# Thresholds of query blocks 3 and 4 by a bit search on ScalarE in a hybrid sparse and sliding-window decoder layer

## Chip, cores and metric

The kernel runs on one core of a Trainium2 chip. The metric is the device time of one execution in microseconds, as the median of several runs. The engines are TensorE (PE, with its weight loads PEld), VectorE (DVE), ScalarE (ACT), GpSimd (POOL) and SyncE (SP), which issues the loads.

## What is computed

One decoder layer of width 1024 over 1024 tokens with 16 meta tokens in front: a SwiGLU FFN as a half step, then a sparse and a sliding-window attention in parallel, merged by sigmoid gates, then a second SwiGLU FFN. The part that the change touches is the selection of keys in the sparse branch. For each query an indexer scores all admissible keys, and attention runs over the 256 best:

```python
def one_block(args):
    qa_b, qi_b, wi_b, qpos = args
    rel = relu(einsum('bqhd,bsd->bqhs', qi_b, ki))
    score = einsum('bqhs,bqh->bqs', rel, wi_b)
    score = where(admissible, score, NEG_INF)
    top_val, top_idx = lax.top_k(score, topk)      # topk = 256
    ...
    s = where(sel_ok, s, NEG_INF); p = softmax(s)
```

The kernel doesn't gather the selected keys. It turns each block's scores into a bias, 0 for a selected key and -1e30 for any other, and adds it to the attention scores of all keys.

## The kernel before

Queries are cut into eight blocks b = 0 to 7 of 128 rows; block b sees w = 16 + 128 (b + 1) keys, so block 3 has 528 columns and block 4 has 656. After the first FFN a middle stage runs in this program order. For each half x of the tokens: keys (`k_half`), indexer queries (`q_groups`), values (`v_half`), the scores of the half's blocks (`score`, L763), the sliding-window queries, and the four sliding-window blocks (`swa_block`, L897), each of which ends with the product `o` (L884) and the transposed tile `oT` (L891, L892). Then come the sparse queries, the search for the thresholds of blocks 5 to 7 (`search`, L796), and the sparse blocks 0 to 7 (`sparse_block`, L954), with eight calls of `swa_merge` between them, each of which computes gates and the sliding-window branch (tiles `p_gate`, `p_br`) and writes two merged tiles `mg` (L1029). After sparse block 7 the sparse gates and the output projection of both halves follow (`p_gate`, `p_br`, `p_out`).

There are two ways to the bias of a block:

- `by_max` (L784 to L794), for blocks 1 to 4, on DVE alone. A round takes the 8 largest scores of each row (MAX8, L790) and overwrites them by a mark (MATCH_VALUE_LOAD and MATCH_REPLACE8, L791). Blocks 1 and 2 drop their smallest scores in 2 and 18 rounds; blocks 3 and 4 mark their 256 largest in 32 rounds each. One last instruction (L792) turns marks into the bias.
- `search` (L796 to L848) and `select` (L850 to L864), for blocks 5 to 7 together. The search finds each row's 256th largest score bit by bit. A round counts on ACT how many scores exceed a trial value: a Sign with the trial as bias and an accumulator, one for each block (L812). Then three small integer instructions on DVE compare the count (`d`, L815), set the bit (`key`, L829) and make the next trial (`nb`, L827). There are 32 rounds, the sign bit among them, and a closing count on DVE (L837). The 16-bit output of the Signs is not used; it goes to the scratch tile `jk`, of which there is one. `select` then makes the bias from the scores and the threshold in eight DVE instructions (L856 to L864), with two tiles for flags, `gt` (which has the scratch tile's buffer) and `eq`.

The order of instructions in this middle stage is not written out by hand. A scheduler of the framework places them, engine by engine: a work item that comes earlier in the program goes first when its inputs are ready by the scheduler's own reckoning. On the chip each engine then runs its list strictly in order, and waits on semaphores. Buffers of one tag are handed out in program order.

Of the kernel before, what the change touches and what calls it, by code (L numbers as in the profile page):

```python
# [9 lines left out]
F16 = mybir.dt.float16  # L10
# [6 lines left out]
P = 128  # L17
# [4 lines left out]
T = META + SEQ  # L22
# [33 lines left out]
def layer_kernel(ctx: ExitStack, tc: tile.TileContext, xT, gains, wgu1, wd1, win, wvi, wbs, wbw, wout,  # L56
# [5 lines left out]
    ph = {}  # L62
# [787 lines left out]
    def select(b, kth):  # L850
        w = META + P * (b + 1)
        raw = sc[b][0]
        gt = ph["sb"].tile([P, T], F16, tag="jk", name="gt", bufs=1)[:, :w]
        eq = ph["sb"].tile([P, T], F16, tag="eq", name="eq", bufs=1)[:, :w]
        room = small(8, "room")[:, 0:1]
        nc.vector.tensor_scalar(out=gt, in0=raw, scalar1=kth, scalar2=None, op0=ALU.is_gt, op1=ALU.add,  # L856
                                accum_out=room)
        nc.vector.tensor_scalar(room, room, -1.0, float(TOPK), op0=ALU.mult, op1=ALU.add)
        nc.vector.tensor_scalar(eq, raw, kth, None, op0=ALU.is_equal)
        nc.vector.tensor_tensor_scan(eq, eq, eq, 0.0, op0=ALU.add, op1=ALU.bypass)  # L860
        nc.vector.tensor_scalar(eq, eq, room, None, op0=ALU.is_le)
        nc.vector.scalar_tensor_tensor(eq, raw, kth, eq, op0=ALU.is_equal, op1=ALU.mult)
        nc.vector.tensor_add(eq, eq, gt)
        nc.vector.tensor_scalar(raw, eq, -1.0, -NEG, op0=ALU.add, op1=ALU.mult)  # L864
# [122 lines left out]
    def new_oT():  # L987
        return ph["sb"].tile([P, 2, 4, 512], F16, tag="oT", name="oT", bufs=3)
# [12 lines left out]
        return gt, pb  # L1001

    oT_w = []
    for x in range(2):
        k_half(x)
        qi += q_groups((x,), 2, 1)
        if x == 0:
            mix_norm(1, norm_stats(acc, SUB_ALL[1]))
        v_half(x)
        for b in range(4 * x, 4 * x + 4):  # L1010
            if b:
                score(b)
        qs += q_groups((x,), 4, 2)
        oT_w.append(new_oT())
        for b in range(4 * x, 4 * x + 4):
            swa_block(b, qs, oT_w[x])
# [1 line left out]

    vm_sp = v_meta(lambda hh: 0)
    oT_s = [new_oT()]  # L1020
    kth = search((5, 6, 7))
    merged = [[], []]

    def swa_merge(d):
# [12 lines left out]
    swa_merge(0)  # L1037
    swa_merge(1)
    swa_merge(2)
    by_max(3)  # L1040
    sparse_block(3, qa, oT_s[0])
    swa_merge(3)
    by_max(4)
    oT_s.append(new_oT())
    swa_merge(4)
    swa_merge(5)
# [16 lines left out]
    for x in range(2):  # L1063
        mT = []
        for d in range(KD):
            gw, bw = load_w(win[20 + d], 1024), load_w(wbs[d], 512)
            mt = hp([P, 2, 512], F16, "mt")
            gt, pb = gated(x, gw, bw, oT_s[x])
# [11 lines left out]
        for d in range(KD):  # L1080
            w = load_w(wout[d], 1024)
# [120 lines left out]
```

## Time and profile before

| what | value |
|---|---|
| median of three runs | 2032.15 us (2031.77 to 2035.65) |
| profiled execution | 2033.16 us, span of its instructions 2031.1 us |
| mean granted TensorE clock | 0.988 of full speed |
| PE, DVE, ACT, POOL busy | 95%, 80%, 44%, 19% of the span |

The span is what the profile cuts into stages; the rest of the execution, 2 us, lies around it. Busy time is the union of an engine's instructions. The middle stage reaches from about 680 us to 1400 us; the first FFN lies ahead of it and the second behind. In the rows below, `L812` is line 812 of the kernel, `out<-in` are tiles by the program's names, and `128x528` is partitions by columns.

### The profile page before, as it was taken

What the parts mean: (1) busy time and instruction counts of PE and PEld (TensorE: products, weight loads), DVE (VectorE), ACT (ScalarE), POOL (GpSimd) and SP (SyncE); (2) the same over time, 40 slices, a digit from 0 to 9 for tenths busy, and PEclk for the clock granted to TensorE, in tenths of its full rate; (3) what the DMA queues carried; (4) which work ended last, traced back from release to release, by engine and by line L of the source; (5) the groups of instructions that cost most, each with busy time, mean ns of one, the idle gap of its engine ahead of it and who ended that gap; (6) DMA issues with size and microseconds to landing.
All of it is one profiled execution on the core that took longest, in us unless ns stands there. A gap on an engine that the chain in (4) does not pass through costs nothing.

```text
span 2031.1 us, 32839 instructions
## 1 busy us (share of the span) xinstructions
PE 1936.5 (95%) x13080; PEld 1197.3 (59%) x13080; DVE 1627.2 (80%) x2779; ACT 901.0 (44%) x1602; POOL 386.9 (19%) x313
## 2 busy tenths in 40 slices
PE   5899999999999989899999999998899999999997
PEld 4588888888888556454545654444344444444443
DVE  7888788778875799999999964566987787788767
ACT  4433233333323446589885643433433243233232
POOL 3611312221310132221001000002322212312200
PEclk9999999999999999999999999999999999999998
DMA  4011111111113543212020024241112121111213
GB/s 158 11 63 48 58 63 50 55 64 58 48 63 105 183 141 112 99 59 73 17 63 17 27 68 156 78 164 49 34 55 68 48 72 47 63 62 47 76 38 130
DMA packets 58873, 146.95 MB, mean 72 GB/s; under 512 B 7264, under 2 KB 13408, under 8 KB 58720
## 3 DMA queue, kind: packets, MB, share of 16 engines
q1 hardware_dynamic: 58720, 144.86, 22.3%
q8 instruction: 102, 1.67, 0.3%
q14 instruction: 51, 0.42, 0.1%
HBM read 130.01 MB, written 14.76 MB: 71 GB/s over the span
## 4 chain that ended last, share of the span: by engine, by line
PE 70%; DVE 18%; ACT 4%; issue 4%; DMA 2%; POOL 2%; DVEq 0%; SPq 0%; ACTq 0%; POOLq 0%
PE pc L327 14%; PE pd L327 14%; PE pa L327 14%; PE pb L327 7%; PE p_br L999 2%; DVE sc L791 2%; DVE u L222 2%; DVE wsp L131 1%; PE p_gate L147 1%; PE p_gate L145 1%; PE p_gate L146 1%; DVE m L790 1%; PE p_out L146 1%; PE p_out L147 1%; PE p_out L145 1%
## 5 line engine op out<-in xcount | busy, mean ns | idle before, releaser
L327 PEld LDWEIGHTS <-wsp 128*128 128x128 f16 x4176 | 410.0, 98 | 214.2 <-issue 12.3
L327 PEld LDWEIGHTS <-x 128*128 128x128 f16 x3132 | 307.3, 98 | 157.9 <-issue 8.5
L327 PE MATMUL pa<-u,wsp 128*128 128x264 f16 (+1 forms) x1440 | 224.7, 310 | 0.0
L131 DVE SCALAR_TENSOR_TENSOR wsp<-wst,wsp 128x1024 f16<-128x1024 f32 (+2 forms) x130 | 134.8, 1038 | 54.6 <-ACT wsp L130 54.3
L130 ACT ACTIVATE wsp<-wst 128x1024 f16<-128x1024 f32 (+2 forms) x130 | 111.7, 863 | 140.1 <-PE p_out L147 45.9
L147 PEld LDWEIGHTS <-wsp 128*128 128x128 f16 x912 | 90.5, 99 | 94.5 <-issue 12.3
L145 PEld LDWEIGHTS <-wsp 128*128 128x128 f16 x912 | 91.0, 100 | 85.1 <-issue 4.1
L146 PEld LDWEIGHTS <-wsp 128*128 128x128 f16 x912 | 90.7, 99 | 80.2 <-issue 3.9
L327 PE MATMUL pb<-tb,wsp 128*128 128x264 f16 (+1 forms) x720 | 113.7, 312 | 8.1 <-ACT tb L235 5.5
L327 PE MATMUL pc<-tb,x 128*128 128x264 f16 (+1 forms) x720 | 113.9, 313 | 6.6 <-DVE c L458 6.4
L327 PE MATMUL pc<-tb,wsp 128*128 128x256 f16 (+1 forms) x720 | 114.2, 314 | 0.0
L327 PE MATMUL pd<-tb,x 128*128 128x256 f16 (+1 forms) x720 | 110.7, 308 | 0.0
L327 PE MATMUL pd<-u,x 128*128 128x256 f16 (+1 forms) x720 | 110.7, 308 | 0.0
L289 POOL TENSOR_TENSOR t<-g,g 128x512 f32<-128x512 f32 x16 | 25.5, 1595 | 436.0 <-DVE g L494 436.0
L812 ACT ACTIVATE jk<-sc,s5nb 128x784 f16<-128x784 f32 (+2 forms) x93 | 97.9, 1052 | 19.0 <-DVE s5nb L827 15.3
L341 ACT ACTIVATE wsp<-sa 128x1024 f16<-128x1024 f32 (+1 forms) x62 | 60.2, 971 | 103.4 <-DVE sa L393 103.4
L327 PE MATMUL pa<-hid,wsp 128*128 128x264 f16 (+1 forms) x648 | 103.1, 310 | 0.0
L341 ACT ACTIVATE wsp<-wst 128x1024 f16<-128x1024 f32 (+1 forms) x62 | 59.9, 967 | 94.3 <-DMA wst<-in_wgu_dram 49.9
L327 PE MATMUL pd<-hid,x 128*128 128x256 f16 (+1 forms) x648 | 101.6, 308 | 0.0
L147 PE MATMUL p_gate<-u,wsp 128*128 128x512 f16 x256 | 97.0, 379 | 1.4 <-DVE wsp L131 1.4
L145 PE MATMUL p_gate<-u,wsp 128*128 128x512 f16 x256 | 97.0, 379 | 0.0
L146 PE MATMUL p_gate<-u,wsp 128*128 128x512 f16 x256 | 97.0, 379 | 0.0
(234 smaller groups left out, 4147.6 us busy)
## 6 DMA issues: line engine op xcount, KB each, us to landing
wst<-in_wgu_dram SPq DMA_DIRECT2D x88, 512.0 KB, 3.7
wst<-in_win_dram SPq DMA_DIRECT2D x44, 512.0 KB, 3.5
wst<-in_wd_dram SPq DMA_DIRECT2D x48, 384.0 KB, 3.4
wst<-in_wd_dram SPq DMA_DIRECT2D x32, 256.0 KB, 2.7
wst<-in_wout_dram SPq DMA_DIRECT2D x16, 512.0 KB, 4.1
qscr<-ry SPq DMA_DIRECT2D x20, 256.0 KB, 2.1
q<-qscr SPq DMA_DIRECT2D x20, 256.0 KB, 3.0
wst<-in_wbs_dram SPq DMA_DIRECT2D x16, 256.0 KB, 2.7
```

The costliest lines, as they stand in the source:

```text
L130: nc.scalar.activation(sp[:, 0, :n], st[:, :n], AF.Copy, scale=WS)
L131: nc.vector.scalar_tensor_tensor(sp[:, 1, :n], st[:, :n], WS, sp[:, 0, :n], op0=ALU.mult, op1=ALU.subtract)
L145: nc.tensor.matmul(ps, w[:, 0, wcols], xt[:, 0, xcols], start=start, stop=False)
L146: nc.tensor.matmul(ps, w[:, 0, wcols], xt[:, 1, xcols], start=False, stop=False)
L147: nc.tensor.matmul(ps, w[:, 1, wcols], xt[:, 0, xcols], start=False, stop=stop)
L222: nc.vector.tensor_sub(u[k][:, 1, s0:s1], t[:, :w], u[k][:, 0, s0:s1])
L289: nc.gpsimd.tensor_sub(vb(t1), vb(b1), va(a1)[:, :, :wb])
L327: nc.tensor.matmul(ps[:, s, :n], w[:, a, wc], tiles[k][:, y, s * stride:s * stride + n], start=start and k == 0 and j == 0, stop=stop and ...
L341: nc.scalar.activation(sp[:, 0, :n], st[:, :n], AF.Copy, scale=WS)
L791: nc.vector.match_replace(out=raw, in_to_replace=m8, in_values=raw, imm_value=MARK)
L812: nc.scalar.activation(junk[:, :w], sc[b][0], AF.Sign, bias=bias[:, j:j + 1], accum_out=s[:, j:j + 1])
L999: nc.tensor.matmul(pb, bw[:, a, c * P:(c + 1) * P], oT[:, y, c, :], start=c == 0 and n == 0, stop=c == 3 and n == 2)
```

## The change

Blocks 3 and 4 get their thresholds by `search`, one search for each block, called right behind the block's scores. `by_max(3)` and `by_max(4)` are replaced by `select` with these thresholds, at the same places of the program. The flag tile `gt` gets a buffer of its own. Blocks 0 to 2 and 5 to 7 are computed as before. Lines behind the second piece move down by one, those behind the third by three.

```diff
     def select(b, kth):
         w = META + P * (b + 1)
         raw = sc[b][0]
-        gt = ph["sb"].tile([P, T], F16, tag="jk", name="gt", bufs=1)[:, :w]
+        gt = ph["sb"].tile([P, T], F16, tag="gt", name="gt", bufs=1)[:, :w]
...
     oT_w = []
+    kth = {}
...
             if b:
                 score(b)
+                if b in (3, 4):
+                    kth.update(search((b,)))
...
-    kth = search((5, 6, 7))
+    kth.update(search((5, 6, 7)))
...
-    by_max(3)
+    select(3, kth[3])
     sparse_block(3, qa, oT_s[0])
     swa_merge(3)
-    by_max(4)
+    select(4, kth[4])
     oT_s.append(new_oT())
```

The scheduler makes new lists for every engine. Three places show what moves.

**DVE, sliding-window blocks of the second half, around one output `o` (L884).** `m_3` and `m_4` are the 8 largest of blocks 3 and 4, whose scores are `sc_8207` and `sc_9243`; `s5` stands for the search of blocks 5 to 7, `s4` for that of block 4. Before:

```order
L875 TENSOR_TENSOR pts<-ptr,pts 128x512
L815 TENSOR_TENSOR s5d<-s5S,s5thr 128x3
L131 SCALAR_TENSOR_TENSOR wsp<-wst,wsp 128x512
L829 SCALAR_TENSOR_TENSOR s5key<-s5d,s5key 128x3
L791 MATCH_REPLACE sc_8207<-m_3_11877,sc_8207 128x528
L884 TENSOR_TENSOR o<-pv_s,a_rec 128x512
L827 SCALAR_TENSOR_TENSOR s5nb<-s5key,s5flip 128x3
L790 MAX m_3_11880<-sc_8207 128x8
L791 MATCH_REPLACE sc_9243<-m_4_12327,sc_9243 128x656
```

and now:

```order
L912 ISA psw,a_mx<-ps_s,msk_7682,snk_7688 128x256
L912 ISA a_mx 128x1
L815 TENSOR_TENSOR s4d<-s4S,s4thr 128x1
L884 TENSOR_TENSOR o<-pv_s,a_rec 128x512
L829 SCALAR_TENSOR_TENSOR s4key<-s4d,s4key 128x1
L827 SCALAR_TENSOR_TENSOR s4nb<-s4key,s4flip 128x1
```

Between the same kinds of instructions, the small steps of block 4's search stand where rounds of MAX8 and MATCH_REPLACE stood. In the list of the changed kernel all 32 rounds of block 3 and 31 of block 4 stand ahead of the last of these eight outputs. Block 3's selection stands ahead of the fifth output, block 4's ahead of the first output of a sparse block.

**ACT, at the third pair of sparse queries (`ry`, L665), behind the last sliding-window block (`oT`, L891).** Before, the search of blocks 5 to 7 (784, 912 and 1040 columns) is in its sixth round here, the sign bit's counted:

```order
L665 ACTIVATE ry<-rt_10446 128x512
L891 ACTIVATE oT<-otr 128x4x128
L812 ACTIVATE jk,s5S<-sc_9301,s5nb 128x784
L665 ACTIVATE ry<-rt_10453 128x512
L812 ACTIVATE jk,s5S<-sc_9359,s5nb 128x912
L812 ACTIVATE jk,s5S<-sc_9417,s5nb 128x1040
L130 ACTIVATE wsp<-wst 128x1024
```

and now:

```order
L812 ACTIVATE jk,s4S<-sc_9519,s4nb 128x656 x2
L891 ACTIVATE oT<-otr 128x4x128
L812 ACTIVATE jk,s4S<-sc_9519,s4nb 128x656 x2
L665 ACTIVATE ry<-rt_10998 128x512
L812 ACTIVATE jk,s4S<-sc_9519,s4nb 128x656
L665 ACTIVATE ry<-rt_11005 128x512
L130 ACTIVATE wsp<-wst 128x1024
L812 ACTIVATE jk,s5S<-sc_9853,s5z 128x784
L812 ACTIVATE jk,s5S<-sc_9911,s5z 128x912
L812 ACTIVATE jk,s5S<-sc_9969,s5z 128x1040
L130 ACTIVATE wsp<-wst 128x512
```

Its first three Signs, with the trial zero (`s5z`), now stand behind the last Sign of block 4 (`s4nb`, 656 columns).

**DVE, between two merged tiles `mg` ahead of sparse block 4 (`wsp` is the low part of a weight).** Before:

```order
L1029 SCALAR_TENSOR_TENSOR mg<-gt,p_br 128x512
L827 SCALAR_TENSOR_TENSOR s5nb<-s5key,s5flip 128x3
L790 MAX m_4_12402<-sc_9243 128x8
L131 SCALAR_TENSOR_TENSOR wsp<-wst,wsp 128x1024
L791 MATCH_REPLACE sc_9243<-m_4_12402,sc_9243 128x656
L131 SCALAR_TENSOR_TENSOR wsp<-wst,wsp 128x512
L790 MAX m_4_12405<-sc_9243 128x8
L815 TENSOR_TENSOR s5d<-s5S,s5thr 128x3
L791 MATCH_REPLACE sc_9243<-m_4_12405,sc_9243 128x656
L829 SCALAR_TENSOR_TENSOR s5key<-s5d,s5key 128x3
L790 MAX m_4_12408<-sc_9243 128x8
L827 SCALAR_TENSOR_TENSOR s5nb<-s5key,s5flip 128x3
```

and now:

```order
L1032 SCALAR_TENSOR_TENSOR mg<-gt,p_br 128x512
L131 SCALAR_TENSOR_TENSOR wsp<-wst,wsp 128x512
L815 TENSOR_TENSOR s5d<-s5S,s5thr 128x3
L829 SCALAR_TENSOR_TENSOR s5key<-s5d,s5key 128x3
L827 SCALAR_TENSOR_TENSOR s5nb<-s5key,s5flip 128x3
L815 TENSOR_TENSOR s5d<-s5S,s5thr 128x3
L829 SCALAR_TENSOR_TENSOR s5key<-s5d,s5key 128x3
L827 SCALAR_TENSOR_TENSOR s5nb<-s5key,s5flip 128x3
L1032 SCALAR_TENSOR_TENSOR mg<-gt,p_br 128x512
```

The rounds of block 4 are gone, and two rounds of the search of blocks 5 to 7 stand between two merged tiles.

## Rows read from the trace of the kernel before

**Rows 1.** Page, part 1: busy us, share of the span, instructions of each engine

```profile
PE 1936.5 (95%) x13080; PEld 1197.3 (59%) x13080; DVE 1627.2 (80%) x2779; ACT 901.0 (44%) x1602; POOL 386.9 (19%) x313
```

**Rows 2.** Timeline of DVE, ends of the stages: start us, us, line, operation

```profile
910.40 0.68 DVE L884 TENSOR_TENSOR o<-pv_s,a_rec 128x512 f32<-128x512 f32 x1
...
1079.90 0.16 DVE L847 TENSOR_TENSOR s5kth<-s5key,s5flip 128x3 int32<-128x3 int32 x1
...
1188.05 0.68 DVE L884 TENSOR_TENSOR o<-pv_b,b_rec 128x512 f32<-128x512 f32 x1
```

**Rows 3.** Busy time by stage: PE, PEld, DVE, ACT, POOL, PEclk, DMA share, GB/s

```profile
751.00:910.00 159.00, 145.01 (x1203) 88.55 (x1202) 152.94 (x410) 105.87 (x272) 39.34 (x30) 0.99 0.29 96
910.00:1080.00 170.00, 163.69 (x1106) 84.51 (x1105) 163.47 (x495) 146.43 (x321) 17.01 (x46) 1.00 0.14 46
1080.00:1188.00 108.00, 104.97 (x1103) 66.84 (x1102) 99.73 (x254) 65.19 (x128) 9.96 (x26) 1.00 0.09 28
```

**Rows 4.** Waits in stage B: us in total, times, longest us

```profile
ACT jk L812 <- DVE s5nb L827: 13.2, 8, 2.7
```

**Rows 5.** Stages A and B, search's flag tile alone: DVE, ACT, PEclk, DMA, GB/s

```profile
751.00:910.00 159.00, 0.00 (x0) 17.15 (x30) 0.99 0.29 96
910.00:1080.00 170.00, 3.51 (x6) 92.76 (x162) 1.00 0.14 46
```

**Rows 6.** DVE groups of stage A: count, busy us, mean ns, idle before

```profile
L790 DVE MAX8 m<-sc 128x8 f32<-128x528 f32 x10 | 7.0, 696 | 0.0
...
L790 DVE MAX8 m<-sc 128x8 f32<-128x656 f32 x2 | 1.7, 830 | 0.0
...
L815 DVE TENSOR_TENSOR s5d<-s5S,s5thr 128x3 int32<-128x3 f32 x5 | 1.4, 289 | 0.0
...
L827 DVE SCALAR_TENSOR_TENSOR s5nb<-s5key,s5flip 128x3 int32<-128x3 int32 x4 | 1.2, 304 | 0.0
...
L829 DVE SCALAR_TENSOR_TENSOR s5key<-s5d,s5key 128x3 int32<-128x3 int32 x4 | 0.6, 151 | 0.0
```

**Rows 7.** Timeline of DVE in stage B, rounds of blocks 3 and 4 beside the search

```profile
996.58 0.16 DVE L815 TENSOR_TENSOR s5d<-s5S,s5thr 128x3 int32<-128x3 f32 x1
996.65 0.85 DVE L790 MAX8 m<-sc 128x8 f32<-128x656 f32 x1
997.41 0.15 DVE L829 SCALAR_TENSOR_TENSOR s5key<-s5d,s5key 128x3 int32<-128x3 int32 x1
997.47 0.72 DVE L790 MAX8 m<-sc 128x8 f32<-128x528 f32 x1
998.09 0.15 DVE L827 SCALAR_TENSOR_TENSOR s5nb<-s5key,s5flip 128x3 int32<-128x3 int32 x1
998.15 0.10 DVE L791 MATCH_VALUE_LOAD sc<-m,sc 128x8 f32 x1
998.22 0.84 DVE L791 MATCH_REPLACE8 sc<-m,sc 128x656 f32<-128x656 f32 x1
998.96 0.09 DVE L791 MATCH_VALUE_LOAD sc<-m,sc 128x8 f32 x1
999.03 0.70 DVE L791 MATCH_REPLACE8 sc<-m,sc 128x528 f32<-128x528 f32 x1
999.64 0.85 DVE L790 MAX8 m<-sc 128x8 f32<-128x656 f32 x1
```

**Rows 8.** Timeline of GpSimd and DVE in stage A

```profile
889.58 1.27 POOL L664 TENSOR_TENSOR rt<-rt,rt 128x512 f32<-128x512 f32 x1 [8.11 <-DVE s5key L829]
...
890.10 0.76 DVE L827 SCALAR_TENSOR_TENSOR s5nb<-s5key,s5flip 128x3 int32<-128x3 int32 x1
```

**Rows 9.** ACT groups of stage B by shape

```profile
L974 ACT ACTIVATION_READ_ACCUMULATOR psp<-psp,b_ng 128x1 f32 x38 | 7.5, 197 | 0.0
...
L974 ACT ACTIVATE psp<-psp,b_ng 128x656 f32<-128x656 f32 x7 | 5.9, 840 | 0.0
```

**Rows 10.** DVE group of one selection, 784 columns

```profile
L860 DVE TENSOR_TENSOR_SCAN eq<-eq 128x784 f16<-128x784 f16 x1 | 1.8, 1782 | 0.0
```


## Prediction

> **What bounds the kernel now.** I read the page first, then the busy time by stage, then the groups and the timeline of the stages that the change touches, and last the waits. The page says that PE is busy 95% of the span [rows 1], but that is an average over stages. The change touches the middle stage alone, from the scores of block 3 to the end of the sparse attention. I cut it at three instructions of DVE [rows 2]: the last output of the sliding-window blocks (910.4), the thresholds of blocks 5 to 7 (1079.9), and the output of sparse block 7 (1188.1). With 751, where block 3's scores end, as its start, this gives stage A (159 us), B (170 us) and C (108 us). The reader should see in [rows 3] that the stages have different limits. In A, DVE is busy 152.9 of 159 and ACT only 105.9. In B, DVE is busy 163.5 of 170, and ACT already 146.4. In C it is PE, 105.0 of 108. So DVE is the engine without room in A and in B. B ends with the search for blocks 5 to 7: its last instruction is the one at 1079.9, and sparse blocks 5, 6 and 7 follow it. ACT's signs of this search waited 13.2 us in B for the trial threshold [rows 4], which stood on DVE behind long max8 rounds.
>
> **Where the removed work lies.** Most of the 64 rounds stand in B, not in A: A holds 10 rounds of block 3 and 2 of block 4 [rows 6], so B holds 52. One round costs DVE, from start to start in [rows 7], 0.62 + 0.07 + 0.61 = 1.30 us at 528 columns and 0.76 + 0.07 + 0.74 = 1.57 us at 656. That is 16.1 us out of A and about 75 us out of B. The two closing mask instructions go too, under 1 us together.
>
> **Where the added work lies.** Each search is 32 rounds of one sign count on ACT and three one-column instructions on DVE. The order of the changed kernel puts all 32 rounds of block 3 and 31 of block 4's ahead of the last sliding-window output, so 63 rounds come into stage A, which has no room on DVE, and the gain falls into stage B. That is the whole case, and each stage has to be priced by itself.
>
> **Stage A, DVE.** The three small instructions have no row at one column; the nearest are those of the present search at three columns. Where nothing is in the way, the next instruction starts 0.07, 0.06 and 0.06 us after them [rows 7]: 0.19 us a round, 12 us for 63 rounds, the lower end. The upper end is their mean durations within A, with no overlap: 0.289 + 0.304 + 0.151 = 0.744 us [rows 6], 47 us. I take A's own means less the overlap of some 0.09 us each that [rows 7] show, 0.48 us a round, 30 us, because they are the same instructions in the same stage. To this come the selection of block 3 and the closing count. The longest of a selection's eight instructions takes 1.8 us at 784 columns [rows 10]; scaled to 528 columns it is 1.2, and I estimate the whole at 4 us, with two further passes of over half that length and five short ones. The closing count and its small steps I estimate at 1 us. Out go the 16.1 us and the four rounds of the search for blocks 5 to 7 that A holds now, 2 us. Net: 30 + 5 - 16 - 2 = +17 us. A has 6 us in which DVE is idle [rows 3]; I let them take their share, so A becomes **11 us longer**. Ends: 0 (free small instructions that fit in the idle time) and +27 (no overlap: 47 + 5 - 16 - 3 = +33, less the 6).
>
> A row that speaks for the upper part: one of these small instructions took 0.76 us in place of 0.15, and it ended at 890.86, when the GpSimd addition that began at 889.58 and took 1.27 us ended [rows 8]. The Trainium skill says of it (SBUF — State Buffer, Terms) that DVE and GpSimd share one port pair, that one instruction holds it for its full length, and that the other engine is fully blocked. By that rule, with a GpSimd that is busy a quarter of A, the small steps would wait more often than my price has it; this trace shows the single case above.
>
> **Stage A, ACT.** The sign counts at 528 and 656 columns have no row either, but an Exp with the same operands and an accumulator has, at 656 columns: 0.84 us, and 0.20 us for the accumulator's read [rows 9]. Taken for both widths, which is a little too much for block 3, 63 x 1.04 = 65 us come, and the 17.2 us of the other search go [rows 5]: 105.9 - 17.2 + 65 = 154 us of 159. ACT stands off the path today; afterwards it would be as full as DVE. What is queued behind a late sign on ACT are the exponentials and copies of the sliding-window blocks, for which PE's next transposes wait. I add nothing for this, since 154 fits into 159 + 11, but it makes a shorter A less likely.
>
> **Stage B.** 75 us leave DVE and some 5 us of block 4's selection come, so DVE is no longer its limit. But the big search starts later. All searches write their sign output into one scratch buffer and take it in program order, so the search for blocks 5 to 7 begins when that of block 4 has ended. Today 27 of its rounds lie in B (162 instructions, six to a round) and cost ACT 92.8 us, 3.44 us a round [rows 5]. In the changed order all 32 lie in B: 110 us. ACT's other work there is 146.4 - 92.8 = 53.6 us and stays. The sum is 164 us, so **ACT takes DVE's place as the limit of B**, and B cannot fall under 164 (-6). ACT idles 23.6 us in B today, 13.2 of them for the late trial threshold [rows 3, 4]; those should go with the max8 rounds, the other 10.4 stay: 174 us, **4 us longer**. The upper end is today's share of 86%: 164 / 0.86 = 190 (+20). PE cannot run ahead of the search, since the rounds stand between its evacuations on DVE's in-order queue: two rounds come between two merged outputs there, and a trial that is late holds the output behind it.
>
> **Stage C and the rest.** C keeps its instructions; PE is its limit and has 3 us left. I take 0, with ends -2 and +5, as block 4's attention may be less far at C's start. The loads, the buffer of its own for the flags `gt` and the row operations of blocks 1 and 2 cost nothing: they lie under PE or DVE as before, and if the new buffer were missing, the selections would only wait for the scratch buffer, a microsecond each.
>
> **Sum.** +11 +4 +0 = +15 us on the profiled execution's 2033.16 gives 2048; that execution is 1.0 us over the median of 2032.15, so I forecast **2047 us**.
>
> **Rivals.**
> *Faster.* The one-column steps slip into DVE's idle time (A +0), and without the max8 rounds the big search runs at ACT's full rate (B -6), with C at -2: 2033 - 8 - 1 = 2024. For it: 75 us less on the engine that is full in B, and a net relief of DVE over A and B together of some 50 us. Against it: this relief lies in B, where ACT needs 164 us for itself. It decides at a sum of A and B under -4 us: B under 166 with A at +2 or less.
> *No change.* A loses 5 and B wins 5: about 2032. This needs the small steps at 0.3 us and an ACT without gaps in B.
> *Slower by more, through GpSimd.* GpSimd is busy 39.3 of A's 159 us [rows 3]. If each of the 189 small steps meets one of its instructions one time in four and waits half of 1.27 us, that is 30 us more than the free 12: 42 + 5 - 16 - 3 = +28, less the idle 6 is +22, with B at +4: 2033 + 26 - 1 = 2058. For it stands [rows 8]; against it that many of A's other DVE instructions already take these waits, so that the same GpSimd time cannot be paid twice. The rule of the Trainium skill quoted above (SBUF — State Buffer, Terms) would have it so.
> *The change doesn't do what it says.* The thresholds could come too late for sparse blocks 3 and 4. The order speaks against this: block 3's mask stands before the first sliding-window output of the second half, block 4's before the first sparse output. I give it nothing.
>
> **Numbers.** Under 0.2% (4 us) a measurement of this kernel can't tell a difference from none. Faster by more: 0.20, the first rival. Within: 0.14. Slower: 0.66, of which 0.46 is my own case between +5 and +25 and 0.20 the GpSimd case and a B near its upper end. The range leaves out what needs all upper ends at once: from 2024 (the first rival) to 2066 (A +20, B +15).
>
> **What would show it.** In the profile after: the last sliding-window output at about 921 instead of 910, with DVE still over 95% busy before it and ACT over 90%; after that DVE at some 100 of 174 us and ACT at over 160; the first signs of the big search at 925 to 930, its rounds 4.9 to 5.4 us apart, and its thresholds at about 1095; the stretch from there to the last sparse output again 108 us. The forecast is wrong if the sliding-window output stays at 910, or if the search needs less than 165 us after it. If the thresholds come late and the end does not, PE had other work, and the reading of B as a chain is wrong.

## Result and profile after

| | before | changed kernel |
|---|---|---|
| median | 2033.76 us (2031.77 to 2035.65, 4 runs) | 2081.9 us (2079.79 to 2084.28, 4 runs) |
| ratio | | 1.0237, 95% interval 1.0217 to 1.0257 |
| stage A, 751 to the last sliding-window output | 159.4 us | 177.2 us (+17.8) |
| stage B, to the thresholds of blocks 5 to 7 | 169.5 us | 185.2 us (+15.7) |
| stage C, to the output of sparse block 7 | 108.2 us | 121.5 us (+13.3) |

The change costs 48 us where 15 were forecast. The three stages add up to +46.8 us, which is the whole difference of the two spans (2078.0 against 2031.1); what follows stage C has the same length. The page's first part, which answers to [rows 1]:

```profile
PE 1951.9 (94%) x13080; PEld 1201.4 (58%) x13080; DVE 1586.4 (76%) x2819; ACT 951.8 (46%) x1730; POOL 383.5 (18%) x313
```

The ends of the three stages in DVE's timeline, as in [rows 2]:

```profile
928.19 0.68 DVE L884 TENSOR_TENSOR o<-pv_s,a_rec 128x512 f32<-128x512 f32 x1
...
1113.42 0.15 DVE L847 TENSOR_TENSOR s5kth<-s5key,s5flip 128x3 int32<-128x3 int32 x1
...
1234.89 0.69 DVE L884 TENSOR_TENSOR o<-pv_b,b_rec 128x512 f32<-128x512 f32 x1 [0.81 <-PE pv_b L879]
```

Busy time by stage of the changed kernel, columns as in [rows 3]:

```profile
751.00:928.20 177.20, 150.05 (x1206) 88.84 (x1205) 169.92 (x570) 136.56 (x367) 38.59 (x32) 0.99 0.26 84
928.20:1113.40 185.20, 165.10 (x1008) 85.73 (x1006) 104.33 (x354) 161.24 (x341) 15.97 (x41) 0.93 0.14 46
1113.40:1234.90 121.50, 118.05 (x1214) 73.09 (x1211) 105.34 (x277) 70.82 (x141) 8.04 (x29) 1.00 0.09 28
```

Beside [rows 3] this shows four things. DVE is relieved in B as forecast (163 to 104 us), and B is longer all the same. ACT takes 161 us of B, also as forecast, but it idles 24 us and not 10. The granted clock of PE in B is 0.93, where it was 1.00. And PE's instructions have moved: B has 1008 matmuls instead of 1106, C has 1214 instead of 1103, so C grew because B left work over. Over A to C, PE was busy 413.8 of 437.1 us before (145.4 + 163.2 + 105.2 with the stages cut at the same instructions) and is now busy 433.2 of 483.9. So of the 46.8 us, **27.4 are PE's added idle time and 19.4 its added busy time** for nearly the same number of matmuls; the lower clock in B alone, 0.07 of 165 us, accounts by estimate for some 12 of these. The stages begin at a fixed time, 751. The last instruction of block 3's scores (L780, `sc`) starts at 751.6 in the kernel before and at 754.0 in this execution, so 2.4 of A's 17.8 us lie ahead of A; in all runs but steps_only it starts between 750 and 754, and A's figures carry that much.

Where PE loses it is seen in slices of 20 us early in B. Before, 940 to 1000:

```profile
940.00:960.00 20.00, 20.00 (x145) 10.18 (x144) 19.32 (x67) 19.98 (x53) 1.37 (x7) 1.00 0.13 41
960.00:980.00 20.00, 19.80 (x157) 10.84 (x156) 19.90 (x63) 19.74 (x45) 1.59 (x8) 1.00 0.01 2
980.00:1000.00 20.00, 19.89 (x104) 9.43 (x103) 20.00 (x50) 14.68 (x29) 0.00 (x0) 1.00 0.12 40
```

The changed kernel, 940 to 1020:

```profile
940.00:960.00 20.00, 14.32 (x76) 6.90 (x75) 17.39 (x52) 14.21 (x33) 6.16 (x7) 0.83 0.36 118
960.00:980.00 20.00, 19.15 (x134) 10.34 (x133) 11.06 (x51) 20.00 (x56) 1.85 (x10) 1.00 0.04 15
980.00:1000.00 20.00, 15.00 (x104) 9.20 (x103) 11.24 (x44) 19.16 (x46) 1.34 (x7) 0.74 0.00 1
1000.00:1020.00 20.00, 17.27 (x110) 9.76 (x109) 11.53 (x39) 19.76 (x44) 0.98 (x5) 0.83 0.13 40
```

Before, PE was full at full clock beside a full DVE and a nearly full ACT. Now there are two different places. In the slice from 940 DVE is nearly full and ACT is not, and PE stands still for most of 942.7 to 949.9:

```profile
945.18 0.20 PE L879 MATMUL pv_b<-vt,ptb 128*128 128x64 f16 x1 [2.43 <-ACT ptb L874]
...
947.28 0.30 PE L756 MATMUL ps_a<-k,q 128*128 128x144 f16 x2 [1.68 <-DMA q<-qscr]
...
948.63 0.34 PE L879 MATMUL pv_b<-vt,ptb 128*128 128x64 f16 x3 [0.62 <-DVE ptb L875]
949.92 0.29 PE L879 MATMUL pv_b<-vt,ptb 128*128 128x64 f16 x2 [0.95 <-DVE ptb L875]
```

It waits for a copy on ACT that stands behind the first three counts of the big search, for the load of a sparse query, and for a step on DVE behind block 4's selection. From 980 to 1020 DVE is little more than half busy, ACT is full, PE has 15 to 17 of 20 us, and its clock falls. PE's timeline there shows what it does:

```profile
983.02 0.31 PE L879 MATMUL pv_b<-vt,ptb 128*128 128x64 f16 x5
984.07 0.44 PE L872 MATMUL ptr<-ident,psp 128*128 128x128 f32 x2 [0.74 <-ACT psp L974]
984.34 0.31 PE L872 MATMUL ptr<-ident,pm 128*128 128x128 f32 x1
985.28 0.50 PE L756 MATMUL ps_a<-k,q 128*128 128x400 f16 x2 [0.63 <-DVE b_mx L970]
...
991.29 0.82 PE L756 MATMUL ps_a<-k,q 128*128 128x400 f16 x2 [0.78 <-DVE b_mx L970]
```

These are the small products of sparse blocks 1 and 2, behind waits for ACT's exponentials or for DVE's maxima; no matmul of a gate stands between them. After these waits the same pair of 400 columns takes 0.82 us instead of 0.50. The waits of B, which answer to [rows 4], name what DVE was waiting for:

```profile
DVE s5d L815 <- ACT jk L812: 35.0, 18, 4.6
DVE psp L970 <- PE ptr L872: 15.4, 16, 2.2
...
ACT jk L812 <- DVE s5nb L827: 11.9, 15, 4.5
```

DVE waited 1.6 us for counts in B of the kernel before. It waits 35.0 us now, with everything behind on its list, the maxima of the sparse blocks among it.

For stage A, the small steps and the counts by shape (count | busy us, mean ns | idle before):

```profile
L827 DVE SCALAR_TENSOR_TENSOR s3nb<-s3key,s3flip 128x1 int32<-128x1 int32 x31 | 9.6, 311 | 0.0
L815 DVE TENSOR_TENSOR s3d<-s3S,s3thr 128x1 int32<-128x1 f32 x32 | 7.2, 224 | 0.5 <-ACT jk L812 0.2
L829 DVE SCALAR_TENSOR_TENSOR s3key<-s3d,s3key 128x1 int32<-128x1 int32 x31 | 6.8, 219 | 0.0
L815 DVE TENSOR_TENSOR s4d<-s4S,s4thr 128x1 int32<-128x1 f32 x27 | 6.4, 235 | 3.7 <-ACT jk L812 3.1
```

```profile
L812 ACT ACTIVATE jk<-sc,s3nb 128x528 f16<-128x528 f32 x31 | 22.6, 731 | 13.7 <-DVE s3nb L827 12.5 <-DVE pm L945 1.1
L812 ACT ACTIVATE jk<-sc,s4nb 128x656 f16<-128x656 f32 x26 | 21.7, 836 | 5.7 <-DVE s4nb L827 5.2 <-DVE a_ng L916 0.2
L812 ACT ACTIVATION_READ_ACCUMULATOR jk<-sc,s3nb 128x1 f32 x31 | 5.8, 189 | 0.0
```

A holds 59 rounds of the two searches (32 and 27 of the compare), not 63: five rounds of block 4 stand behind the last sliding-window output, where the text ahead of the prediction counted one.

### The profile page after: what moved, and what is told of

The parts are those of the page before. It is cut to its first block, busy times and chain, and to the rows that moved or that the text cites. A ratio compares the mean times of both kernels' runs of the same rounds, so it can differ in the third digit from the quotient of the medians.

```text
span 2078.0 us, 33048 instructions
## 1 busy us (share of the span) xinstructions
PE 1951.9 (94%) x13080; PEld 1201.4 (58%) x13080; DVE 1586.4 (76%) x2819; ACT 951.8 (46%) x1730; POOL 383.5 (18%) x313
## 4 chain that ended last, share of the span: by engine, by line
PE 67%; DVE 17%; ACT 9%; issue 3%; DMA 2%; POOL 1%; DVEq 0%; SPq 0%; ACTq 0%; POOLq 0%
PE pc L327 14%; PE pd L327 14%; PE pa L327 14%; PE pb L327 7%; ACT jk L812 5%; PE p_br L999 2%; DVE u L222 2%; DVE wsp L131 2%; PE p_out L146 1%; PE p_out L147 1%; PE p_out L145 1%; PE p_gate L146 1%; PE p_gate L145 1%; PE p_gate L147 1%; PE pv_b L879 1%
## 5 line engine op out<-in xcount | busy, mean ns | idle before, releaser
L131 DVE SCALAR_TENSOR_TENSOR wsp<-wst,wsp 128x1024 f16<-128x1024 f32 (+2 forms) x130 | 132.5, 1020 | 62.1 <-ACT wsp L130 61.8
L327 PE MATMUL pc<-tb,x 128*128 128x264 f16 (+1 forms) x720 | 115.4, 316 | 6.9 <-DVE c L458 6.7
L812 ACT ACTIVATE jk<-sc,s5nb 128x784 f16<-128x784 f32 (+2 forms) x93 | 97.9, 1053 | 12.6 <-DVE s5nb L827 11.9
```

The costliest lines, as they stand in the source:

```text
L131: nc.vector.scalar_tensor_tensor(sp[:, 1, :n], st[:, :n], WS, sp[:, 0, :n], op0=ALU.mult, op1=ALU.subtract)
L327: nc.tensor.matmul(ps[:, s, :n], w[:, a, wc], tiles[k][:, y, s * stride:s * stride + n], start=start and k == 0 and j == 0, stop=stop and ...
L812: nc.scalar.activation(junk[:, :w], sc[b][0], AF.Sign, bias=bias[:, j:j + 1], accum_out=s[:, j:j + 1])
```

## Experiments

All runs, with the stages of their profiled execution cut at the same instructions. Each ratio is to runs of the kernel before that were timed beside it; their medians lie between 2032.4 and 2034.3. The profiled execution is one of those timed and can lie some us off the median, 5.6 below it for short_signs.

| run | median us | ratio, 95% interval | A | B | C |
|---|---|---|---|---|---|
| before | 2032 to 2034 | | 159.4 | 169.5 | 108.2 |
| changed | 2081.9 | 1.0237 (1.0217 to 1.0257) | 177.2 | 185.2 | 121.5 |
| b_one_round | 2055.8 | 1.0115 (1.010 to 1.013) | 160.4 | 143.6 | 157.1 |
| one_round_merges | 2044.7 | 1.0063 (1.0045 to 1.0081) | 158.8 | 143.0 | 145.6 |
| one_round_spread | 2039.0 | 1.0025 (1.0015 to 1.0036) | 161.8 | 144.6 | 139.6 |
| merges_before | 2034.3 | 1.001 (1.0001 to 1.002) | 161.0 | 173.2 | 106.8 |
| before_spread | 2035.5 | 1.0006 (0.9997 to 1.0015) | 158.5 | 169.5 | 108.5 |
| act_mask | 2033.7 | 1.0001 (0.9993 to 1.001) | 160.0 | 169.4 | 108.7 |
| only3 | 2048.6 | 1.0079 (1.0064 to 1.0094) | 168.8 | 166.6 | 115.4 |
| only4 | 2051.5 | 1.0096 (1.008 to 1.0111) | 164.1 | 192.2 | 97.3 |
| joint34 | 2065.3 | 1.0159 (1.0142 to 1.0176) | 174.1 | 188.0 | 106.4 |
| joint_merges | 2055.8 | 1.011 (1.0095 to 1.0126) | 176.4 | 190.7 | 99.2 |
| merges_between | 2064.9 | 1.0157 (1.0142 to 1.0172) | 179.3 | 192.0 | 99.9 |
| after_spread | 2064.8 | 1.0153 (1.0139 to 1.0166) | 177.5 | 192.2 | 98.0 |
| late_567 | 2067.2 | 1.017 (1.0154 to 1.0186) | 175.6 | 200.6 | 102.6 |
| short_567 | 2061.1 | 1.014 (1.0125 to 1.0155) | 175.6 | 106.9 | 181.3 |
| short_signs | 2058.9 | 1.013 (1.0113 to 1.0147) | 167.7 | 172.1 | 118.6 |
| no_steps | 2080.9 | 1.0238 (1.0223 to 1.0254) | 183.1 | 144.1 | 158.1 |
| steps_only | 2065.6 | 1.0163 (1.0149 to 1.0177) | 167.0 | 145.5 | 156.5 |
| own_junk | 2080.8 | 1.0235 (1.0219 to 1.0252) | 176.6 | 184.8 | 121.4 |

Two theories stood against each other at the start. By the prediction's, DVE bounds A and B: taking the max8 rounds away helps B, and the loss is the price of what was added. By its rival, PE sets the end all along, had little idle time to give, and loses wherever the new order leaves it without work.

### Is the relief of DVE worth anything

**b_one_round**, in the kernel before:

```diff
-        for r in range((w - TOPK if drop else TOPK) // 8):
+        for r in range(1 if b in (3, 4) else (w - TOPK if drop else TOPK) // 8):
```

> The kernel before, with one round instead of 32 for blocks 3 and 4 (its thresholds are wrong, the rest of the work is there). It takes 62 of 64 rounds, some 88 us, off DVE and puts nothing in their place. If DVE bounds stages A and B, as the prediction read them, the end comes 15 to 30 us earlier (2003 to 2018), since B could fall from 170 us to ACT's 146 or to PE's 164. If PE was the limit of B all along and DVE merely busy beside it, the relief is worth little: 2024 to 2034.

Measured: 2055.8 us, **23 us slower with 62 rounds less to do**. Neither theory had this. The stages behind A:

```profile
911.40:1055.00 143.60, 132.90 (x849) 67.45 (x848) 79.92 (x282) 132.73 (x291) 15.97 (x40) 0.95 0.13 44
1055.00:1212.10 157.10, 146.48 (x1366) 88.19 (x1364) 120.56 (x308) 78.77 (x156) 6.35 (x32) 0.97 0.10 31
```

The thresholds come 25 us earlier than before (1055 against 1080), and sparse block 7 ends 24 us later. So B is no chain on which the end hangs. PE did 849 matmuls until the thresholds instead of 1103 and had to do the rest afterwards, with a hole in PE's timeline between two neighbours:

```profile
1071.62 0.38 PE L146 MATMUL p_gate<-u,wsp 128*128 128x512 f16 x1
1080.56 0.72 PE L756 MATMUL ps_a<-k,q 128*128 128x336 f16 x2 [8.55 <-DVE b_mx L970]
```

In that hole the selections of blocks 5, 6 and 7 stand in one row on DVE (1055 to 1078), ahead of the maxima of sparse block 4. A changed by only 1.0 us, although DVE was relieved of 10 us there. The order of the lists changed too, so this run alone doesn't part the worth of the relief from the price of the order.

### Merges as work for PE

In the lists, the kernel before wrote four merged outputs `mg` ahead of sparse block 2's output, the changed one two. **merges_between** puts the first three merges between the sparse blocks; **one_round_merges** does it to the kernel of the last section, **merges_before** to the kernel before.

```diff
     sparse_block(0, qa, oT_s[0])
+    swa_merge(0)
     sparse_block(1, qa, oT_s[0])
+    swa_merge(1)
     sparse_block(2, qa, oT_s[0])
-    swa_merge(0)
-    swa_merge(1)
     swa_merge(2)
```

> The changed kernel with the first three merges of the sliding-window branch, which are PE work that needs little of ACT and DVE, put in the program between sparse blocks 0, 1 and 2 instead of behind all three. If the loss in B is PE without other work while ACT is full, this gives PE work there: 10 to 25 us come back (2057 to 2072). If ACT or DVE bound B by their sums, the order of PE's work does nothing: 2077 to 2087.

Measured: 2064.9, 17 us back. Matmuls of the gates alone between 985 and 1001 (PE, ACT, clock, DMA share, GB/s), in the changed kernel:

```profile
985.00:1001.00 16.00, 0.00 (x0) 0.00 (x0) 0.68 0.00 1
```

and with the merges between:

```profile
985.00:1001.00 16.00, 7.84 (x29) 1.19 (x2) 1.00 0.01 2
```

ACT is as full as it was (19.95 of 20 us from 980 to 1000), so a full ACT does not by itself hold PE back; PE without other work beside it does. A and B are longer than in the changed kernel (179.3 and 192.0), and C is 21.6 us shorter. The hole from 942 on is not cured: the slice 940 to 960 has PE busy 14.96 us at clock 0.83 here, and 14.91 at 0.83 in late_567 below.

> The kernel with one round for blocks 3 and 4 (its thresholds are wrong), and the first three merges put between sparse blocks 0, 1 and 2. That kernel lost 23 us although it had 88 us less work on DVE. If it lost them because PE had no merges to do while ACT was full early in B, they come back: 2033 to 2042. If the loss is the run of selections on DVE behind the thresholds (8.6 us of idle PE there) and the clock behind it, most of it stays: 2046 to 2056.

Measured: 2044.7, in between the two: 11 of the 23 us come back, the rest has another cause.

> The control: the kernel before with the same move of the first three merges. There the merges already stand between the sparse blocks in PE's list (five merged outputs ahead of sparse block 2's output, against two in the changed kernel), so the move should do nothing: 2027 to 2037. If the move is worth 17 us here too, it is an improvement of its own and says nothing on the change.

Measured: 2034.3, a ratio of 1.001: no gain. The move cures something that the change brought. (The expectation says five merged outputs where the trace has four.)

### The row of selections

**one_round_spread** is one_round_merges, with the selections of blocks 6 and 7 made to wait for the ends of sparse blocks 4 and 5; **after_spread** and **before_spread** are merges_between and the kernel before with the same edit, in `sparse_block`:

```diff
         nc.vector.reciprocal(rec, sm)
+        if b in (4, 5):
+            late = mcst([P, 1], F32, f"late{b}", 1)
+            nc.vector.scalar_tensor_tensor(late, rec[:, 0:1], 0.0, kth[b + 2], op0=ALU.mult, op1=ALU.add)
+            kth[b + 2] = late
         finish(pv, rec, oT, b)
```

> The kernel with one round for blocks 3 and 4 (its thresholds are wrong) and the merges between, and in addition the selections of blocks 6 and 7 made to wait for the end of sparse blocks 4 and 5 (one more one-column instruction each). Twelve us of its 23 are left to explain; its trace has one hole of PE behind the thresholds, where the three selections stand in a row on DVE ahead of sparse block 4's maxima (8.6 us in the kernel with one round alone), and a lower clock behind it. If that is the rest, 8 to 12 us come back: 2032 to 2037. If not, it stays at 2042 to 2048.

Measured: 2039.0, between the two cases. Against the runs of before beside each, the loss falls from 12.3 to 4.7 us. In one_round_merges, the slice behind the thresholds is

```profile
1060.00:1080.00 20.00, 13.16 (x115) 8.12 (x114) 19.41 (x45) 5.38 (x13) 0.76 (x3) 0.83 0.13 40
```

and with the selections spread

```profile
1060.00:1080.00 20.00, 19.76 (x175) 11.99 (x173) 16.41 (x48) 10.65 (x24) 1.19 (x6) 1.00 0.13 41
```

So of the 23 us that the missing rounds cost, 18 come back by two changes of the order: three merges (11) and two selections (8). Some 5 us stay open, and in none of these orders is the kernel without the rounds faster than before.

> The changed kernel with the merges between and the selections of blocks 6 and 7 spread in the same way. Its hole behind the thresholds was 3.1 us, so 2 to 5 us come back from the 2065 with the merges alone: 2060 to 2063. More would say that the row of selections costs more than the idle time shows.

Measured: 2064.8, the same as merges_between: this hole is no part of the changed kernel's loss, or it only moved.

> The kernel before with the selections of blocks 6 and 7 spread in the same way. From 1080 to 1120 its DVE is full and PE idles a microsecond in 20, so 0 to 2 us are to be had: 2030 to 2034. A gain beyond that would be a kernel better than both.

Measured: 2035.5, no difference (1.0006). **act_mask** tries stage C of the kernel before in another way:

```diff
-        nc.vector.tensor_scalar(raw, eq, -1.0, -NEG, op0=ALU.add, op1=ALU.mult)
+        nc.scalar.activation(raw, eq, AF.Copy, scale=-NEG, bias=NEG)
```

> The kernel before with the last of the eight instructions of a selection, the one that writes the bias, on ACT instead of DVE (blocks 5 to 7). From 1080 to 1120 DVE is full (19.95 and 19.96 of 20 us), ACT has 9 to 11 us of 20, and PE idles about a microsecond in 20. If DVE sets the pace there, up to 2 us come back: 2029 to 2032. If PE is the limit there too, nothing: 2031 to 2035.

Measured: 2033.7, a ratio of 1.0001: nothing. But DVE's busy time in C falls only from 99.7 to 98.8 us, so this is a small test of what relief is worth there.

### The big search in stage B

**short_567** shortens the counts of blocks 5 to 7, with the count that a trial is compared to set to match:

```diff
-                nc.scalar.activation(junk[:, :w], sc[b][0], AF.Sign, ...
+                u = 16 if b > 4 else w
+                nc.scalar.activation(junk[:, :u], sc[b][0][:, :u], AF.Sign, ...
```

> The changed kernel with the sign counts of blocks 5 to 7 over 16 columns only (so their thresholds are wrong): some 60 us less on ACT, nearly all behind the last sliding-window output. If PE starves in the first 100 us of B because the counts hold up the exponentials and copies of sparse blocks 0 to 3 on ACT, PE's granted clock stays at 1.00 there, B and C together shrink by 20 us or more, and the end is under 2060. If the holes of PE come from DVE's order, less than 10 us come back: over 2070.

Measured: 2061.1, 21 us back; B and C together take 288.2 us instead of 306.7, and the clock ahead of the thresholds is 0.97: near the first case, but short of it in each number. The thresholds come 80 us earlier (1033 against 1113), and the end only 21: three quarters of what the search gives up is not on the path.

```profile
926.60:1033.50 106.90, 96.65 (x630) 49.27 (x627) 75.95 (x293) 76.22 (x304) 15.25 (x33) 0.97 0.18 58
1033.50:1214.80 181.30, 178.39 (x1587) 104.23 (x1587) 131.16 (x340) 90.22 (x179) 7.29 (x37) 1.00 0.10 32
```

Behind them PE is busy 178.4 of 181.3 us at full clock: there PE is the limit.

**late_567** calls the search behind the first three merges:

```diff
-    kth.update(search((5, 6, 7)))
...
     swa_merge(2)
+    kth.update(search((5, 6, 7)))
     select(3, kth[3])
```

> The changed kernel with the search for blocks 5 to 7 called behind the first three merges instead of ahead of the sparse blocks, so that the scheduler prefers sparse blocks 0 to 2 to its counts. If early B is lost because the counts stand ahead of the exponentials of these blocks on ACT, PE's granted clock stays near 1.00 from 930 to 1020 and up to 20 us come back: 2060 to 2075. Against that the thresholds come later: if B is ACT's sum, as the prediction had it, every delay of the search moves the end: 2085 to 2100.

Measured: 2067.2, 15 us back, although the thresholds come 14 us later (1127). From 980 to 1020 the clock is back at 1.00:

```profile
980.00:1000.00 20.00, 19.86 (x135) 9.89 (x133) 9.47 (x28) 18.39 (x39) 0.59 (x3) 1.00 0.13 41
1000.00:1020.00 20.00, 18.86 (x90) 8.59 (x89) 6.15 (x19) 18.05 (x33) 0.00 (x0) 1.00 0.12 40
```

So from 980 to 1020 it is the counts' place ahead of the exponentials of sparse blocks 0 to 2 that starves PE, and giving PE either of them earlier or a merge in between helps. Of the 13.2 us between the two profiled spans only 5.1 are gained by the end of C; the other 8.1 lie behind it, where 835.0 us remain instead of 843.1 and PE has 8.3 us less to do, so some products that otherwise stand behind C seem to be done ahead of its end.

**own_junk** gives the scratch output of the searches of blocks 3 and 4 another buffer:

```diff
-                junk = ph["sb"].tile([P, T], F16, tag="jk", name="jk", bufs=1)
+                junk = ph["sb"].tile([P, T], F16, tag="gt" if n == 1 else "jk", name="jk", bufs=1)
```

> The changed kernel with the scratch output of the searches of blocks 3 and 4 in another buffer than that of blocks 5 to 7 (block 3's selection then comes behind block 4's search). The prediction held that the shared buffer makes the search of blocks 5 to 7 wait for block 4's. If so, it starts 10 us or more earlier, and up to 10 us come back: 2070 to 2078. If not the buffer but ACT's list sets its start, nothing changes: 2078 to 2086.

Measured: 2080.8, nothing, but the run doesn't answer its question. It moves only the counts on ACT; the closing counts of blocks 3 and 4 on DVE (L837) still write `jk`, and the first count of the big search waits for block 4's:

```profile
938.64 0.95 ACT L812 ACTIVATE jk<-sc,s5z 128x784 f16<-128x784 f32 x1 [0.33 <-DVE jk L837]
```

In the changed kernel it starts right behind the same closing count too (940.93). Whether the buffer or the order of ACT's list makes the big search start late is open.

### Stage A and the two blocks apart

**only3** and **only4** change one block alone (`if b == 3:` and `if b == 4:` in place of `if b in (3, 4):`, and `by_max` kept for the other).

> The changed kernel with only block 3 by search, block 4 by max8 as before. If the loss comes from counts and small steps in A, in proportion to the rounds, this costs half of the 48 us: about 2057. If it comes from the search of blocks 5 to 7 that starts late behind block 4's, block 3's search alone lets that one start nearly as before and costs 8 to 15 us: 2042 to 2048.

> The changed kernel with only block 4 by search, block 3 by max8 as before. If the loss goes by the rounds: about 2057. If it is the late start of the search of blocks 5 to 7, block 4's search alone brings most of the loss: 2062 to 2075.

Measured: 2048.6 and 2051.5. Block 3 by itself costs A 9.4 us and C 7.2, and B is 2.9 us shorter; most of the late start of the big search comes with block 4 (first trial at 859 before, 873 with block 3 alone, 933 with block 4 alone). But block 4 alone costs 18.6 us, not the 30 to 42 expected, and the two sum to 34 where both together cost 48. So the loss goes neither in proportion to the rounds nor by the start of the big search alone.

**joint34** makes one search of the two, behind block 4's scores:

```diff
-                if b in (3, 4):
-                    kth.update(search((b,)))
+                if b == 4:
+                    kth.update(search((3, 4)))
```

> The changed kernel with one search for blocks 3 and 4 together, behind block 4's scores. The sign counts on ACT stay the same 64; DVE's small steps are halved (32 rounds instead of 64, two columns instead of one). If the small steps in A are the cost, some 20 us come back: 2055 to 2066. If ACT's counts or the late start of the search of blocks 5 to 7 are the cost, it stays at 2072 to 2085.

Measured: 2065.3. Some 17 us come back, but hardly in A, where the steps were halved: DVE's busy time in A falls to 148.6 us, and A stays at 174.1. C is 15 us shorter, at 106.4; why, no run tells. **joint_merges** adds the merges between:

> The changed kernel with one search for blocks 3 and 4 together and with the first three merges between sparse blocks 0 to 2. Alone these gave back 17 us each, in different stages by the reading (A's steps, B's PE work), so together 30 to 35 us: 2046 to 2054. If both only cured the same hole in early B: 2058 to 2066. Under 2033 would be a better kernel than before; PE's busy time in A to C of before leaves too little for that.

Measured: 2055.8, between the two cases. The gains overlap: 17 us each alone, 26 together.

**short_signs** shortens the counts of blocks 3 and 4 in the way of short_567 (`u = 16 if b in (3, 4) else w`).

> The changed kernel with the sign counts of blocks 3 and 4 over 16 columns only (so their thresholds are wrong): the same number of counts and small steps, the same chain, but each count shorter by roughly half, some 30 us less on ACT. If the length of the counts on ACT is what costs, 15 us or more come back: 2055 to 2067. If it is the small steps on DVE or the place of the work, it stays within 8 us of 2082.

Measured: 2058.9, 23 us back: A 9.5 shorter, B 13.1 (the search of block 4 now ends inside A, and the big search starts at 925 instead of 948), C 2.9. A again:

```profile
751.00:918.70 167.70, 147.99 (x1197) 86.78 (x1195) 165.34 (x574) 113.87 (x373) 38.05 (x29) 0.99 0.27 89
```

With ACT nearly as free as before (113.9 us against 105.9) and all small steps in place, A is still 8.3 us longer than before, and DVE is full (165.3 of 167.7). Taken from that last instruction of block 3's scores, A is 158.8 us before, 168.2 here (it starts at 750.5) and 174.2 in the changed kernel. So 8 to 9 us go with the steps on DVE and the closing work, and 6 to 9.5 with the length of the counts on ACT, as far as one execution of each can tell.

**no_steps** keeps the counts, now in a function `signs`, and takes out what stands between them:

```diff
+        if n == 1:
+            for k in range(32):
+                signs(zero)
+            return {b: zero[:, j:j + 1] for j, b in enumerate(bs)}
         d = accept(zero)
```

> The changed kernel with all 64 sign counts of blocks 3 and 4 on ACT, at full length, but without the small steps on DVE between them and without the closing count (so their thresholds are wrong). If the 42 us of small steps in A are the cost of A, A falls back to 160 to 165 us and the end to 2055 to 2067. If the counts on ACT are, A stays at 172 to 178. Either way the other half of the loss, which the run with one round showed without any search of blocks 3 and 4 (+23 us), should stay: not under 2050.

Measured: 2080.9, and A is 183.1: longer, not shorter. Without the steps nothing paces the counts, and they run in a block on ACT while PE waits and loses its clock:

```profile
840.00:860.00 20.00, 12.72 (x59) 5.73 (x57) 12.87 (x24) 19.15 (x49) 0.00 (x0) 0.74 0.00 0
860.00:880.00 20.00, 14.91 (x58) 6.14 (x57) 12.40 (x17) 19.09 (x41) 5.79 (x5) 0.66 0.31 106
```

**steps_only** does the opposite: the counts are skipped for blocks 3 and 4, and the compare reads a constant.

> The changed kernel with the small steps of blocks 3 and 4 on DVE (compare, set, next trial, 32 rounds each, reading a constant) but without their 64 counts on ACT and without the closing count (so their thresholds are wrong). A's 18 us are either the steps on DVE, which was full before, or the counts on ACT, which take 55 us there. If the steps: A stays at 170 us or more. If the counts, or the waits between counts and steps: A comes back to 160 to 165. The end follows A and keeps what the missing max8 rounds cost in B and C (+23 us by the run with one round): 2050 to 2058 in the second case, 2064 or more in the first.

Measured: 2065.6, A 167.0. This run doesn't answer its question: with no count to wait for, the steps moved ahead of stage A (689 to 729 us). The last instruction of block 3's scores then starts at 759.8 instead of 751.6, and from there to the last sliding-window output it is 158.2 us, as before (158.8): all that A shows as longer lies ahead of it. Both runs show again that work left out lets the order shift, so a part's price can't simply be read from leaving the part out.

No kernel here is faster than the one before.

## Why the prediction was wrong

The direction was right, the size and the mechanism were not: 2047 with a range to 2066 was forecast, 2082 came.

**The step that failed** is the reading of the stages: "DVE is the engine without room in A and in B", with ACT to take its place as the limit of B, and C untouched. A full engine is not yet the limit. In B before, PE stood at 163.7 of 170 us at full clock [rows 3], as full as DVE (163.5), and the prediction passed over it. Taking 89 us (31 rounds at 1.30 and 31 at 1.57, [rows 7]) off DVE returned nothing and cost 23 (b_one_round). All idle time that PE had in A to C was 23 us; with PE's work there unchanged, that was the most that any relief could bring. The Trainium skill (Perfetto Trace Analysis, Identifying the Most-Contended Engine) would have the engine of highest occupancy optimized first, with PE judged by its share of the peak rate and by its weight loads and not by its matmul time. This case speaks against it: weight loads were busy 84.5 of 170 us, which looks like half of PE free, and yet taking work off DVE won nothing; the matmul time of 163.7 us at clock 1.00 was the nearer sign.

**Stage A, +11 forecast, +17.8 measured.** The net of DVE was +17 in the working and +16.6 by the busy time (153.3 to 169.9): right, though with 59 rounds, whose steps last 0.71 us a round where 63 at 0.48 were forecast; the durations overlap with other instructions, so 0.71 is more than they add. Wrong was the share of 6 us that DVE's idle time was to take: 7.3 us idle remain. Wrong also was "I add nothing" for ACT, because its sum fitted: the sum did fit (136.6 of 177.2; 154 was forecast), and the length of the counts still costs some 6 to 9.5 us (short_signs).

**GpSimd, the rival for more.** Its mechanism is there. In A of the changed kernel 23 of 178 small steps last over 0.25 us; each of them overlaps a GpSimd instruction and ends with it, and together they take 15.3 us more than 0.155 us each. The first two of them, in the timelines of GpSimd and DVE:

```profile
758.13 1.36 POOL L666 TENSOR_TENSOR ry<-rt,ry 128x512 f16<-128x512 f32 x1 [0.74 <-ACT ry L665]
758.40 1.11 DVE L827 SCALAR_TENSOR_TENSOR s3nb<-s3key,s3flip 128x1 int32<-128x1 int32 x1
...
760.79 1.26 POOL L664 TENSOR_TENSOR rt<-rt,rt 128x512 f32<-128x512 f32 x1 [1.29 <-DVE s3d L815]
760.98 1.08 DVE L829 SCALAR_TENSOR_TENSOR s3key<-s3d,s3key 128x1 int32<-128x1 int32 x1
```

The rival had one step in four wait for 0.64 us; it was one in eight, for 0.66. The rule of the Trainium skill quoted in the prediction (SBUF — State Buffer, Terms) agrees with these rows. The prediction's "single case" was not single: the kernel before has a second one in A (0.85 us at 898.15) and two in B, and the means of 0.289 and 0.304 us behind its own price hold those of A already. The price lies inside the net that was forecast for DVE, so it does not explain the miss. No run here takes GpSimd's work away.

**Stage B, +4 forecast, +15.7 measured.** ACT's sum was 164 and is 161.2. The trial thresholds come 5.0 us apart (30 intervals from 948.5 to 1098.8), within the forecast of 4.9 to 5.4. The term that failed is ACT's idle time: 13.2 us of it were to go with the max8 rounds and did not; ACT still waits 11.9 us for the big search's trials and 5.6 for block 4's, because DVE, relieved, now waits 35.0 us for counts and holds up all that is queued behind. The late start is real (first count at 940.9, where 925 to 930 was forecast); that the shared scratch buffer causes it, as the prediction has it, is neither shown nor refuted (own_junk).

**Stage C, 0 forecast, +13.3 measured.** C took over 110 matmuls that B had not done. The sentence at the end of the prediction, that B as a chain would be wrong if thresholds and end came apart, is what the runs show: thresholds 25 us earlier with the end 24 later (b_one_round), 80 earlier with the end 21 earlier (short_567), 14 later with the end 15 earlier (late_567, more than half of it gained behind C).

**What carries the loss instead.** Without max8 rounds between them, the lists bring the counts of the big search, sparse blocks 0 to 2 and few merges together early in B. ACT is full, DVE waits for counts, and PE has only products that wait for both. Changes of order alone show this for a part of the loss: merges_between gives back 17 of the 48 us, with merges_before as the control, late_567 gives 15, and one_round_spread shows it for the selections. joint_merges, which halves the small steps too, gives back 26; no run that keeps both searches removes the other 22. How the scheduler came to prefer this order no run tells. Open are the exact split of A's 18 us, the hole from 942 to 950, some 5 us of b_one_round, what joint34 gains in C, and why the two blocks together cost 14 us more than the sum of each.

## What to carry to other kernels

Before work is moved off a full engine, leave it out altogether and time that: if the kernel doesn't get faster without the work, a cheaper way of doing it is unlikely to help, unless the new order of what is left is to blame. Look for the engine whose idle time is smallest over the whole stretch and at full clock, not for each stage's fullest; its idle time is about all there is to win while its own work stays the same. Where a scheduler fixes each engine's order, work that was taken out also takes away the spacing of what stood between it, and the first thing to read in the new profile is what the limiting engine was doing beside the stretch that became denser.

## What was not expected of the hardware

PE's clock can fall without a long pause of PE. From 982 to 990 in the changed kernel no pause was longer than 0.8 us. Up to 988 PE was busy 1.2 to 1.3 of every 2 us, with transposes and products of 64 to 512 columns, some of them behind waits of up to 0.8 us, and the granted clock was still 1.00. From 988 to 990 it was 0.72, then 0.50, the lower of the two levels (1.2 of 2.4 GHz):

```profile
986.00:988.00 2.00, 1.32 (x9) 0.41 (x8) 0.57 (x2) 2.00 (x5) 0.00 (x0) 1.00 0.00 0
988.00:990.00 2.00, 1.22 (x7) 1.21 (x7) 1.09 (x4) 2.00 (x7) 0.42 (x2) 0.72 0.00 0
...
994.00:996.00 2.00, 2.00 (x20) 1.53 (x19) 1.16 (x6) 1.23 (x4) 0.21 (x1) 0.50 0.01 4
996.00:998.00 2.00, 1.94 (x14) 1.28 (x11) 1.59 (x6) 2.00 (x7) 0.00 (x0) 0.50 0.00 0
...
1000.00:1002.00 2.00, 0.87 (x11) 0.49 (x10) 1.29 (x4) 2.00 (x4) 0.00 (x0) 1.00 0.00 0
```

It was back at 1.00 from 1000 on, behind 4 us in which PE was busy almost throughout, and fell again soon after. At the lower level the same products take longer, so the busy share itself rises (7.92 of 10 us from 990 to 1000). With gates in between, the 16 us from 985 to 1001 ran at 1.00. Small holes thus cost more than their length: by the estimate above, some 12 us of B's loss are the clock.
